# Decayed keys made token-major by VectorE block transposes and a pass through HBM, in a hybrid encoder block

## The chip, the core and the metric

The kernel runs on one core of a Trainium2 chip. The core has TensorE (matrix products, written PE in the profile; its weight loads are PEld), VectorE (DVE), ScalarE (ACT), GpSimd (POOL) and SyncE (SP), which here issues the DMAs. Each engine works through its own instructions in order and waits on semaphores for the others. The metric is the device time of one execution in microseconds (us); less is better.

## What is computed

One layer of a bidirectional hybrid encoder on 1024 tokens of width 1024: gated linear attention (GLA) in both directions beside a pooling branch, both gated and merged, then a SwiGLU feed-forward part. The change touches the attention alone. Per head (4 heads, key width 128, value width 256) and direction:

```python
b = jnp.cumsum(log_a, axis=3)               # per chunk of tokens
q_e = q * jnp.exp(b)
k_e = k * jnp.exp(-b)
scores = jnp.einsum('bhncd,bhnsd->bhncs', q_e, k_e)   # masked afterwards
o_intra = jnp.einsum('bhncs,bhnse->bhnce', scores, v)
kv = jnp.einsum('bhnsd,bhnse->bhnde', k_d, v)         # k_d = k * exp(b_last - b)
# state: dec_n * state + kv_n, over the chunks in turn
o_inter = jnp.einsum('bhncd,bhnde->bhnce', q_e, s_in)
```

The backward direction is the same on reversed tokens without the diagonal, and both outputs are added. For `scores` the decayed keys are needed with the feature on the partitions (feature-major); for `kv` the sum runs over the tokens, so they are needed with the token on the partitions (token-major).

## The kernel before

**Precision.** Most products take float32 operands in two parts, a rounded high part and the rest as the low part. `split_to` (L199) makes them: a ScalarE copy to the high part (L200), a subtraction for the low part (L201). `products` (L270) then issues three matmuls for one product: high by high, high by low, low by high. So a product of token-major keys `kt` and values `v` needs the high part of `kt` for its first two matmuls and the low part for the third.

**The order.** All instructions are written out by hand in program order; nothing reorders them. The long projections (`feature_major`, L296, and others) form the main stream on TensorE. After each product of that stream `mm3` (L275) calls `pump` (L161), which lets side work go on: the generators put into `side` with `begin`, one of which is `attention(h)` (L813). Such a generator yields a number, the count of main-stream products of 512 columns that go by before its next piece. Head h+1's projections of q and k run on the main stream while head h's attention is at the side. Weight loads and jobs that prepare later weights hang on the same pump (`pending`, `aside`).

**A head's attention.** Tokens come in two halves of 512 (`half`), the direction is `d` (0 forward, 1 backward), and a (half, d) pair is called a group here. The groups are taken in the order (1,1), (0,1), (0,0), (1,0):

- `decay` (L842): VectorE subtracts, runs the cumulative sum (a scan of 512 columns) and takes off the chunks' totals.
- `exponentials` (L865): ScalarE makes the two exponentials and the factors.
- `apply_decay` (L876): VectorE writes the decayed keys `ke` (L881), GpSimd the decayed queries `qe`.
- `transposed_keys` (L896): TensorE transposes the four 128x128 blocks of `ke[half][:, d, :]` into one PSUM bank `kp` (L899), and `split_to` reads that bank into `kt` (L901).
- `advance` (L904): for one chunk n of 128 tokens, the product `kv` of `kt` and `value(n)`, then the running state on VectorE (`st`, L911 or L913) and its two scaled copies on ScalarE (`sb` or `sf`, L917; `so`, L921). The backward states go from n = 7 down to n = 1 (L967), with the first four steps on `kts[1, 1]` and the rest on `kts[0, 1]`; the forward states go up from n = 0 inside the loop at L985, on `kts[0, 0]` and from n = 4 on `kts[1, 0]`.
- `scores` (L924): the products of `ke` and `qe`, masked and split.

Where the four groups are transposed and split before: (1,1) at L954, three units after `apply_decay(0, 1)`; (0,1) at L959, 4.5 units later and 2.5 units ahead of step n = 7; (0,0) after step n = 3 (L976); (1,0) after the output of chunk 0 (L1005).

**Buffers.** `slots` is a pool of 39 buffers of 4 KB per partition, which a great many things share (`ke`, `qe`, `kt`, values, states, loaded tensors). PSUM has eight banks: three for the main stream, five (`ps_g`) for everything at the side, `kp` among it. `raw` is a ring of four buffers for loaded weights. All loads and stores are issued by SP, in program order, a waiting one ahead of all behind it.

## Time and profile before

| what | us |
|---|---|
| median of 3 runs (1374.78 to 1375.9) | 1375.06 |
| span of the profiled execution | 1373.4 |
| TensorE busy in the span | 1361.4 |
| VectorE, ScalarE, GpSimd busy | 836.8, 647.3, 752.1 |
| the 64 transposes into `kp`, busy on TensorE | 9.6 |
| first and last of them, start | 89.1 and 301.6 |

How to read the rows of the profile: `L273 PE MATMUL ps<-hh,wh` is line 273 of the kernel, the engine, the operation, and what it writes and reads by the program's names with buffer numbers left out. A row of a group ends with the busy time, the mean duration of one in ns and the engine's idle time ahead of them, with what ended it. A row of a timeline begins with the start and the duration in us; `x4` says that four like instructions are merged, and `[1.16 <-ACT kt L200]` that the engine stood idle for 1.16 us until ScalarE's instruction of that name. A row of windows gives the stretch, its length, the busy time of PE, PEld, DVE, ACT and POOL with their counts, the granted TensorE clock (1.00 is full), the busy share of the DMA engines, and GB/s. Rows of DMA issues give what is written and read, the count, the size of one, and the median us from issue to landing. SPq is SP's queue of DMA issues. Matmuls are pipelined and overlap, so their cost in the stream is read from the distance of starts.

### The profile page before, as it was taken

To read this page: it belongs to the slowest core of one execution; us is meant where nothing else is said; L and a number is where in the kernel's file an instruction comes from. 1 tells how busy PE (TensorE), PEld (TensorE's weight loads), DVE (VectorE), ACT (ScalarE), POOL (GpSimd) and SP (SyncE) were. 2 spreads that over 40 slices of the span, in tenths; PEclk is the share of its full clock that TensorE was granted. 3 is DMA by queue.
4 is the path that set the end of the run, shared out by engine and by line. 5 is a ranking of instruction groups with operands and counts; after the bars stand their busy time and mean duration, and the time that the engine had idled before them with its cause. 6 is when DMAs were issued, how large, how long until landed. Compare 5 with 4: busy or idle time off the path is not lost. (4 is left out here: it accounts for less than half of the span.)

```text
span 1373.4 us, 17879 instructions
## 1 busy us (share of the span) xinstructions
PE 1361.4 (99%) x6310; PEld 1132.9 (82%) x6310; DVE 836.8 (61%) x1034; ACT 647.3 (47%) x1177; POOL 752.1 (55%) x557
## 2 busy tenths in 40 slices
PE   9999999999999999999999999999999999999998
PEld 7888888888888888888888888888888888888886
DVE  6974556554735777678883955655566556343375
ACT  7365666755534445554346533333333334444253
POOL 3323723222597547667764376666676667455454
PEclk9999999999999999999999999999999999999999
DMA  6321523314778569995416355555544447985451
GB/s 227 113 87 52 181 90 92 95 60 123 245 236 278 186 198 308 373 386 216 150 71 241 112 174 176 176 176 177 176 145 137 146 136 266 384 301 187 169 215 77
DMA packets 167834, 251.97 MB, mean 183 GB/s; under 512 B 11160, under 2 KB 94144, under 8 KB 167744
## 3 DMA queue, kind: packets, MB, share of 16 engines
q1 hardware_dynamic: 167600, 250.57, 53.8%
q8 instruction: 49, 0.80, 0.2%
q14 instruction: 41, 0.34, 0.1%
q10 hardware_dynamic: 144, 0.26, 0.0%
HBM read 168.74 MB, written 82.05 MB: 183 GB/s over the span
## 5 line engine op out<-in xcount | busy, mean ns | idle before, releaser
L201 POOL TENSOR_TENSOR wl<-fs,wh 128x512 fp32r<-128x512 f32 x124 | 173.1, 1400 | 163.5 <-ACT wh L200 104.0
L273 PE MATMUL ps<-gh,wh 128*128 128x512 f32 x616 | 240.5, 390 | 0.0
L273 PE MATMUL ps<-gl,wh 128*128 128x512 f32 x616 | 239.8, 389 | 0.3 <-DVE gl L1691 0.3
L273 PE MATMUL ps<-gh,wl 128*128 128x512 f32 x616 | 239.7, 389 | 0.0
L201 POOL TENSOR_TENSOR wl<-fraw,wh 128x512 fp32r<-128x512 f32 x93 | 134.0, 1442 | 75.0 <-ACT wh L200 72.4
L201 POOL TENSOR_TENSOR ol<-gor,oh 128x1024 fp32r<-128x1024 f32 (+1 forms) x42 | 101.3, 2417 | 86.0 <-ACT oh L200 71.7
L273 PE MATMUL ps<-hh,wh 128*128 128x512 f32 x356 | 145.1, 408 | 0.7 <-ACT ga L1474 0.7
L273 PE MATMUL ps<-hh,wl 128*128 128x512 f32 x356 | 139.0, 390 | 0.0
L273 PE MATMUL ps<-hl,wh 128*128 128x512 f32 x356 | 138.8, 390 | 0.0
L273 PEld LDWEIGHTS ps<-gl,wh 128*128 128x128 f32 x616 | 115.7, 188 | 24.5 <-DVE gl L1691 0.7
L273 PEld LDWEIGHTS ps<-gh,wh 128*128 128x128 f32 x616 | 115.7, 188 | 24.1 <-ACT hb L1710 0.2
L273 PEld LDWEIGHTS ps<-gh,wl 128*128 128x128 f32 x616 | 115.7, 188 | 23.9
L273 PE MATMUL ps<-oh,oh 128*128 128x512 f32 x308 | 119.8, 389 | 0.0
L273 PE MATMUL ps<-ol,oh 128*128 128x512 f32 x308 | 119.8, 389 | 0.0
L273 PE MATMUL ps<-oh,ol 128*128 128x512 f32 x308 | 119.8, 389 | 0.0
L201 POOL TENSOR_TENSOR wl<-wraw,wh 128x512 fp32r<-128x512 f32 x56 | 92.3, 1679 | 44.7 <-ACT wh L200 44.6
L201 POOL TENSOR_TENSOR wl<-raw,wh 128x512 fp32r<-128x512 f32 x34 | 47.4, 1404 | 108.3 <-ACT wh L200 71.9
L201 DVE TENSOR_TENSOR ol<-wor,oh 128x1024 fp32r<-128x1024 f32 (+1 forms) x42 | 62.8, 1506 | 68.1 <-ACT oh L200 55.5
L200 ACT CAST wh<-fs 128x512 fp32r<-128x512 f32 x124 | 76.1, 615 | 29.5 <-DVE fs L1093 28.3
L273 PEld LDWEIGHTS ps<-hh,wl 128*128 128x128 f32 x356 | 66.8, 188 | 14.4
L273 PEld LDWEIGHTS ps<-hh,wh 128*128 128x128 f32 x356 | 67.0, 188 | 13.1 <-ACT ga L1474 1.1
L273 PEld LDWEIGHTS ps<-hl,wh 128*128 128x128 f32 x356 | 67.0, 188 | 12.0
(281 smaller groups left out, 3073.4 us busy)
## 6 DMA issues: line engine op xcount, KB each, us to landing
fraw<-in_w_ffn_in_dram SPq DMA_DIRECT2D x44, 512.0 KB, 6.1
gor<-g_out SPq DMA_DIRECT2D x35, 512.0 KB, 6.1
fraw<-in_w_in_dram SPq DMA_DIRECT2D x22, 512.0 KB, 6.5
g_out<-s SPq DMA_DIRECT2D x44, 256.0 KB, 2.3
wor<-t_out SPq DMA_DIRECT2D x20, 512.0 KB, 3.7
raw<-in_w_in_dram SPq DMA_DIRECT2D x36, 256.0 KB, 5.1
g_out<-g SPq DMA_DIRECT2D x33, 256.0 KB, 2.6
x<-in_x_dram SPq DMA_DIRECT2D x16, 512.0 KB, 5.6
```

Of the source, the lines that this page charges most:

```text
L200: nc.scalar.copy(hi, src)
L201: eng.tensor_tensor(lo, src, as_f32(hi), op=ALU.subtract)
L273: nc.tensor.matmul(ps, a[i], b[j], start=first and n == 0, stop=last and n == 2, skip_group_check=onto)
```

## The change

`transposed_keys` goes, and with it the 64 transposes on TensorE, the PSUM bank `kp` and the splits that read it. Four functions take its place:

- `turn_keys`: one VectorE transpose of 32x32 blocks over `ke[half][:, d, :]` (128 x 512) into the first half of a slot `kq`, with the blocks' columns rearranged on the way.
- `put_keys`: four DMAs, one for each 32 partitions, store that to a scratch tensor `k_out` in HBM, in rows of 512 bytes, so that the blocks land where a full transpose would have them.
- `get_keys`: one DMA loads the scratch tensor (128 x 512) into the second half of `kq`.
- `split_keys`: `split_to` from there into `kt`, with the columns put back into order on the way.

Each group's steps are spread over the schedule. `turn_keys` follows `apply_decay` of its group. The split of (1,1) moves to where (0,1) was transposed and split before, and that of (0,1) moves behind step n = 6; (0,0) and (1,0) are split where they were transposed before.

```diff
+SQ = 32
...
+    k_out = {
+        (h, half, d): dram.tile([P, HALF], F32, name=f"k_out{h}{half}{d}")
+        for h in range(HEADS) for half in range(2) for d in range(2)
+    }
...
-        def transposed_keys(half, d):
-            kp = bank(ps_g, "kp")
+        turned = {}
+
+        def turn_keys(half, d):
+            both = slot(s="kq")
+            nc.vector.transpose(
+                both[:, 0, :].rearrange("p (j c b) -> p c j b", j=4, b=SQ),
+                ke[half][:, d, :].rearrange("p (c j a) -> p c j a", j=4, a=SQ),
+            )
+            turned[half, d] = both
+
+        def put_keys(half, d):
+            to = k_out[h, half, d].rearrange("(j a) (i m) -> i a j m", a=SQ, i=4)
             for i in range(4):
-                nc.tensor.transpose(kp[:, i * P : (i + 1) * P], chunk_of(ke, 4 * half + i, d), ident[:, :])
+                src = turned[half, d][i * SQ : (i + 1) * SQ, 0, :]
+                nc.sync.dma_start(to[i], src.rearrange("p (j m) -> p j m", j=4))
+
+        def get_keys(half, d):
+            nc.sync.dma_start(turned[half, d][:, 1, :], k_out[h, half, d])
+
+        def split_keys(half, d):
             kt = slot(F32R, s="kt")
-            split_to(kt[:, 0, :], kt[:, 1, :], kp[:, :])
-            return kt
+            hi, lo = (kt[:, i, :].rearrange("p (c i b) -> p c i b", c=4, b=SQ) for i in range(2))
+            back = turned[half, d][:, 1, :].rearrange("p (i c b) -> p c i b", i=4, b=SQ)
+            split_to(hi, lo, back)
+            kts[half, d] = kt
...
+        kts = {}
         decay(1, 1)
         yield HOLD
         exponentials(1, 1)
...
         apply_decay(1, 1)
+        turn_keys(1, 1)
         yield HOLD - 2
         exponentials(0, 1)
         decay(0, 0)
+        put_keys(1, 1)
         yield 2
         apply_decay(0, 1)
+        turn_keys(0, 1)
         yield HOLD - 2
         exponentials(0, 0)
-        kts = {(1, 1): transposed_keys(1, 1)}
+        put_keys(0, 1)
+        get_keys(1, 1)
         yield 1.5
         apply_decay(0, 0)
         decay(1, 0)
+        turn_keys(0, 0)
         yield HOLD - 2
-        kts[0, 1] = transposed_keys(0, 1)
+        split_keys(1, 1)
         exponentials(1, 0)
+        get_keys(0, 1)
+        put_keys(0, 0)
         yield 2.5
...
             if n == 7:
                 apply_decay(1, 0)
+                turn_keys(1, 0)
+            elif n == 6:
+                split_keys(0, 1)
+                get_keys(0, 0)
+            elif n == 5:
+                put_keys(1, 0)
             yield 1.2
             if n == 3:
-                kts[0, 0] = transposed_keys(0, 0)
+                split_keys(0, 0)
+                get_keys(1, 0)
                 yield 0.5
...
             if n == 0:
                 yield 0.38
-                kts[1, 0] = transposed_keys(1, 0)
+                split_keys(1, 0)
```

## The prediction

> **What bounds the kernel now.** I read the page's busy times and chain of waits, then the windows of the four stretches in which the heads' keys are transposed, then the timelines of TensorE, VectorE, ScalarE and the DMA queue (SPq) there. Times are us from the start of the span.

> ```profile
> PE 1361.4 (99%) x6310; PEld 1132.9 (82%) x6310; DVE 836.8 (61%) x1034; ACT 647.3 (47%) x1177; POOL 752.1 (55%) x557
> PE 44%; DVE 1%; ACT 1%; issue 0%; POOLq 0%; POOL 0%; DVEq 0%; ACTq 0%
> 80.00:120.00 40.00, 40.00 (x222) 34.59 (x222) 24.67 (x45) 22.96 (x53) 17.37 (x16) 1.00 0.18 54
> 145.00:185.00 40.00, 39.08 (x217) 33.20 (x215) 22.32 (x41) 23.31 (x54) 24.80 (x22) 1.00 0.41 135
> ```

> TensorE is busy for 99% of the span, and in the first two heads' stretches for 40.00 and 39.08 of 40 us. So the program is one in-order stream of matmuls: what leaves that stream is gained, and each wait that enters it is lost, because nothing later gives it back. VectorE is busy 24.67 and 22.32 of 40 us there, the DMA engines 18% and 41%: room on average. Averages don't decide this change, though. The order within some ten microseconds of each head does.

> **What goes.** Per head four groups of four transposes leave TensorE, 16 groups in all.

> ```profile
> L899 PE MATMUL kp<-ident,ke 128*128 128x128 f32 x64 | 9.6, 272 | 0.0
> 88.45 0.62 PE L273 MATMUL ps<-wv,hh 128*128 128x512 f32 x2
> 88.90 0.40 PE L273 MATMUL ps<-wv,hl 128*128 128x512 f32 x1
> 89.14 0.60 PE L899 MATMUL kp<-ident,ke 128*128 128x128 f32 x4
> 89.50 0.70 PE L273 MATMUL ps<-wv,hh 128*128 128x512 f32 x2
> ```

> They never waited (0.0 idle), so their time is true TensorE time. What one group costs I read from starts, since ends overlap. A 512-wide matmul is normally followed after about 0.23 us (two of them and the next start: 88.45 to 88.90). With a group between, the next one starts 0.60 after 88.90, which is 0.37 more, and the pair after it takes 0.70 where 0.62 is normal: 0.45 us a group. Sixteen make **7.2 us**; the row's 9.6 us busy is the upper end, 16 x 0.37 = 5.9 the lower. The freed PSUM banks gain nothing more: TensorE waits for no bank there.

> **What is moved.** I name a group by (half, direction): (1,1), (0,1), (0,0), (1,0) in order. The split of (1,1) into `kt` stood right behind its transposes. It now stands where the split of (0,1) stood, because the round trip through HBM has to fit in between. But the first `kv` matmuls of a head (n = 7) use (1,1), and their place in TensorE's order is the same. The third of them needs the low part. So I compare, head by head, VectorE's low part of the *second* group with the third `kv` matmul:

> ```profile
> 95.45 0.68 DVE L201 TENSOR_TENSOR kt<-kp,kt 128x512 fp32r<-128x512 f32 x1
> 95.09 0.28 PE L273 MATMUL kv<-vh,kt 128*128 128x256 f32 x1
> 157.70 0.28 PE L273 MATMUL kv<-vh,kt 128*128 128x256 f32 x1
> 222.64 0.68 DVE L201 TENSOR_TENSOR kt<-kp,kt 128x512 fp32r<-128x512 f32 x1
> 222.05 0.28 PE L273 MATMUL kv<-vh,kt 128*128 128x256 f32 x1
> 284.79 0.68 DVE L201 TENSOR_TENSOR kt<-kp,kt 128x512 fp32r<-128x512 f32 x1
> 285.30 0.28 PE L273 MATMUL kv<-vh,kt 128*128 128x256 f32 x1
> ```

> Two groups leave TensorE ahead of these matmuls in each head, so it arrives 0.90 earlier: at 94.19, 156.80, 221.15 and 284.40. The low part at the new place ended at 96.13, 160.18 (row below), 223.32 and 285.47. Without any transfer or added VectorE work TensorE would already wait 1.9 + 3.4 + 2.2 + 1.1 = **8.6 us**, more than is saved.

> **What is added.** Per group: one VectorE transpose of 128x512, four stores of 64 KB, one load of 256 KB, and a split that reads SBUF in place of PSUM.

> ```profile
> L309 DVE TENSOR_SCALAR xn<-x,n1rs 128x1024 f32<-128x1024 f32 (+1 forms) x10 | 7.4, 746 | 4.2 <-POOL n1rs L305 4.1
> L851 DVE TENSOR_TENSOR_SCAN z<-carry,la 128x512 f32<-128x512 bf16 x8 | 14.2, 1772 | 0.3
> L201 DVE TENSOR_TENSOR wv<-vraw,wv 128x512 fp32r<-128x512 f32 x5 | 4.1, 821 | 0.0
> L200 ACT CAST wv<-vraw 128x512 fp32r<-128x512 f32 x8 | 4.8, 618 | 0.9 <-DMA vraw<-in_w_in_dram 0.9
> 116.36 0.34 SPq L694 DMA_DIRECT2D s_out<-wsum  x1
> g_out<-s SPq DMA_DIRECT2D x44, 256.0 KB, 2.3
> wl<-u_out SPq DMA_DIRECT2D x14, 256.0 KB, 3.3
> raw<-in_w_in_dram SPq DMA_DIRECT2D x36, 256.0 KB, 5.1
> ```

> - The transpose isn't in this trace. Bounds: 0.37 us (half of the SBUF scaling of 1024 columns) and 1.77 (the scan). I take 0.69, as for the other one-result-per-column operations of 512 (`ke`, `la`, the `kt` split), which is 0.61 in a full queue, where starts overlap by 0.08.
> - The split: 0.62 for the high part, 0.82 for the low part (the SBUF rows; from PSUM the low part was 0.69).
> - An issue on SP: 0.34, so about 0.37 each, 1.48 for a group's four stores. Load to landing: 2.3 to 5.1 us; I take 3.3, the row of a scratch tensor of the same 256 KB.

> [...]

> Now the path to the first low part, with head 1 in full, then the starts for the others:

> ```profile
> 152.95 0.68 DVE L881 TENSOR_TENSOR ke<-z,k 128x512 f32<-128x512 f32 x1
> 154.79 0.69 DVE L201 TENSOR_TENSOR kt<-kp,kt 128x512 fp32r<-128x512 f32 x1 [1.16 <-ACT kt L200]
> 155.40 0.68 DVE L881 TENSOR_TENSOR ke<-z,k 128x512 f32<-128x512 f32 x1
> 159.16 0.43 DVE L862 TENSOR_TENSOR z<-z,tot 128x256 f32<-128x256 f32 x1
> 159.50 0.68 DVE L201 TENSOR_TENSOR kt<-kp,kt 128x512 fp32r<-128x512 f32 x1
> 88.48 0.68 DVE L881 TENSOR_TENSOR ke<-z,k 128x512 f32<-128x512 f32 x1
> 216.41 0.68 DVE L881 TENSOR_TENSOR ke<-z,k 128x512 f32<-128x512 f32 x1
> 218.34 3.03 SPq L208 DMA_DIRECT2D raw<-in_w_in_dram  x2
> 277.56 0.68 DVE L881 TENSOR_TENSOR ke<-z,k 128x512 f32<-128x512 f32 x1
> ```

> SP runs in order, and the load of (1,1) is queued behind the stores of (0,1), which wait for (0,1)'s transpose. In head 1 `ke` of (0,1) ends at 153.63; two transposes (1,1 and 0,1) push this to 154.85; four stores, 156.33; load landed, 159.63; high part, 160.25; low part, 161.07. TensorE wanted it at 156.80: **4.3 us**. The same sum from 89.16, 217.09 and 278.24 gives 96.60, 224.92 (SP is at the first of two weight loads until 218.70, 0.39 later) and 285.68: waits of 2.4, 3.8 and 1.3. Together **11.8 us**. VectorE alone gives nearly the same in head 1: from 154.85 the queue `ke` to `z` of 4.19 (155.40 to 159.59), a third transpose and the low part end at 160.5. A faster transfer alone saves at most 0.6 there.

> The split of (0,1), moved behind step n = 6, waits next, on ScalarE.

> ```profile
> 159.63 0.60 ACT L871 ACTIVATE qe<-z 128x512 f32<-128x512 f32 x1 [1.42 <-DVE z L862]
> 160.64 0.19 ACT L873 ACTIVATE fac<-tot 128x8 f32<-128x8 f32 x1
> 160.73 0.50 ACT L917 ACTIVATE sb<-st,fac 128x256 f32<-128x256 f32 x1
> 161.13 0.50 ACT L921 ACTIVATE so<-st,fac 128x256 f32<-128x256 f32 x1
> 161.90 0.28 PE L273 MATMUL kv<-vh,kt 128*128 128x256 f32 x1
> 95.36 1.13 ACT L200 CAST wh<-raw 128x512 fp32r<-128x512 f32 x2
> ```

> ScalarE waits for the load in order, so behind the high part (160.25) come the exponentials of (1,0), 1.20 (159.63 to 160.83), then `sb`/`so` of n = 7, 0.90, after `st`; another `st` (some 0.5) and pair, then high and low part of (0,1): about 165.5. Its third matmul (161.90) stands 4.20 behind that of n = 7, so at 165.27: 0.25 us more. In head 0 two weight casts (1.13, last row) stand there too: 1.0 by the same sum. I put about 0.5 on each of heads 2 and 3: **2.2 us** in all. (0,0) and (1,0) have ten units of the schedule or more between load and split and cost nothing; were that cover gone, they would cost like (0,1).

> Queued behind SP's new waits are loads of weights and of `wsum`, and stores. I cost them at nothing: four `raw` buffers, and TensorE itself stands meanwhile. `kq` needs one or two of 39 slots at a time and comes free before the slots get short.

> **Sum.** 1373.4 (span of the profiled execution) - 7.2 + 11.8 + 2.2 = 1380.2. The median of the runs, 1375.06, lies 1.7 above that span, so **1382 us**, 0.5% slower.

> **Rivals.**

> 1. *Hidden (faster).* The low part is there in all heads and only the saving counts: 1375.06 - 7.2 = 1368. For it: VectorE and the DMA engines have room on average. Against it: the 8.6 us by which the new place was late before anything was added. It decides only if VectorE stands idle enough ahead of the split; the 1.16 us idle in head 1's rows goes into the added transposes. 0.10.
> 2. *Balance.* A transpose at 0.37 and a landing at 2.3 us take 0.64 + 1.0, and a low part of 0.69 another 0.13, off each path, 1.8 a head and 1.3 in head 3, together 6.7: 1375. 0.13.
> 3. *Slow transfers.* Stores and `raw` loads both move 512-byte rows; if the load lands after 5.1 us behind its own stores, each head loses 1.8 more: 1382 + 7.2 = 1389, and some weights late behind SP. 0.13.
> 4. *Clock.* In the row below TensorE is idle and the granted clock averages 0.67. A wait that long in heads 1 and 2 could halve the clock for as long again, some 1.7 us of loss each: 1385. 0.04.

> ```profile
> 1368.40:1373.40 5.00, 0.00 (x0) 0.00 (x0) 0.75 (x1) 0.72 (x1) 0.37 (x1) 0.67 0.34 128
> ```

> [...]

> **Chances and range.** Forecast, 1378 to 1387 for itself: 0.60. A run of this kernel tells about 0.2% from no change (1372.3 to 1377.8). Faster 0.10 (rival 1), same 0.13 (rival 2), slower 0.77 (the rest). The range leaves out rival 1 and the far end of rival 3: 1373 to 1391.

> **What would show it.** In the profile after: no `kp`; TensorE waiting in front of `kv`, named by `kt`'s casts and differences, 1 to 4 us in each head, most in heads 1 and 2; ScalarE idle in front of `kt`, ended by the DMA into `kq`; 16 transposes on VectorE near 0.69 us; the busy time of TensorE some 7 us shorter. I'm wrong if `kv` starts without waits (the path is shorter than summed), if the load lands after 2.3 us and VectorE is never full, or if the waits sit at weights (`wl`), which would mean SP's queue did the harm.

## The result, and the profile after

Each time is a median of runs on one chip.

| | before | after |
|---|---|---|
| time | 1374.9 us (1374.7 to 1375.9) | **1392.3 us** (1391.8 to 1392.8) |
| ratio | | 1.0125, 95% interval 1.0110 to 1.0139 |
| span of the profiled execution | 1373.4 us | 1390.7 us |

The forecast was 1382 us, with a range to 1391. The sign was right. The loss is 17.4 us, where 7 were forecast.

From the page of the changed kernel the busy times; from the view of its groups by form (line, engine, operation, count; busy us, mean ns; idle before) the new ones; from the view of DMA issues the trip (count, KB, median us to landing):

```profile
PE 1361.9 (98%) x6246; PEld 1130.0 (81%) x6246; DVE 846.7 (61%) x1050; ACT 647.4 (47%) x1177; POOL 753.4 (54%) x557
```

```profile
L905 DVE STREAM_TRANSPOSE kq<-ke 128x512 f32<-128x512 f32 x16 | 11.3, 709 | 1.2 <-POOL qe L887 0.6
L202 DVE TENSOR_TENSOR kt<-kq,kt 128x512 fp32r<-128x512 f32 x16 | 12.5, 780 | 32.9 <-ACT kt L201 31.4 <-DMA s_out<-wsum 1.5
```

```profile
k_out<-kq SPq DMA_DIRECT2D x64, 64.0 KB, 1.8
kq<-k_out SPq DMA_DIRECT2D x16, 256.0 KB, 3.5
```

The 64 transposes are gone from TensorE (6310 matmuls became 6246), yet its busy time is no shorter: some of the others ran longer. The new operations cost what was forecast: the transpose 0.71 us (0.69), the low part 0.78 (0.82), a load 3.5 from issue to landing (3.3).

The two stretches of the first heads again (TensorE, its loads, VectorE, ScalarE, GpSimd busy; granted clock, DMA share), then the view of waits from 80 to 340 us, which spans the four heads (us in total, times, longest):

```profile
80.00:120.00 40.00, 37.85 (x199) 31.86 (x198) 26.63 (x49) 21.84 (x50) 16.01 (x15) 1.00 0.38 112
145.00:185.00 40.00, 29.81 (x139) 24.83 (x138) 20.51 (x35) 19.41 (x42) 26.20 (x23) 0.87 0.66 191
```

```profile
PE kv L274 <- ACT kt L201: 15.0, 3, 10.0
PE kv L274 <- DVE kt L202: 1.7, 6, 0.6
ACT kt L201 <- DMA kq<-k_out: 11.3, 3, 4.6
ACT kt L201 <- POOL fac L888: 7.3, 1, 7.3
```

In the second stretch TensorE fell from 39.08 to 29.81 us busy, at a clock of 0.87. Over the four heads three waits for the high part of `kt` make 15.0 us, and one of them alone, in head 1, is 10.0 us.

The other matmuls run in the same order in both kernels, so they can be paired. Over all pairs TensorE idles 16.7 us more. It saves 0.43 to 0.46 us at each of the 16 places where a group of transposes went, 7.2 in all. The span grew by 17.3 us, so the rest, 17.3 - 16.7 + 7.2 = 7.8 us, are matmuls that follow each other more slowly. Some 5 of these lie from 168 to 176 and from 236 to 244 us, behind the long waits of heads 1 and 2, where the granted clock is 0.50 to 0.86.

**Head 1.** SP's queue, one ScalarE row and TensorE's rows of n = 7 (start, us, engine, line, operation, count, and in brackets the idle time before it):

```profile
152.02 0.82 SPq L757 DMA_DIRECT2D raw<-in_w_in_dram  x1
152.94 3.49 SPq L915 DMA_DIRECT2D k_out<-kq  x4
159.39 0.34 SPq L695 DMA_DIRECT2D s_out<-wsum  x1
159.83 1.84 SPq L915 DMA_DIRECT2D k_out<-kq  x4
161.84 0.34 SPq L918 DMA_DIRECT2D kq<-k_out  x1
...
167.43 0.62 ACT L201 CAST kt<-kq 128x512 fp32r<-128x512 f32 x1 [7.33 <-POOL fac L888]
...
168.10 0.58 PE L274 MATMUL kv<-vh,kt 128*128 128x256 f32 x1 [9.99 <-ACT kt L201]
169.10 0.58 PE L274 MATMUL kv<-vh,kt 128*128 128x256 f32 x1 [0.20 <-DVE kt L202]
```

The transpose of (0,1) was done at 155.9, but its four stores went out only at 159.83. A store of `s_out` stood ahead of them and waited for one of GpSimd's sums until 159.39. So the load of (1,1) was issued at 161.84; the forecast had 156.33. The high part began at 167.43, which is 5.6 us after the issue, where 3.3 was forecast. So the high part came 7.8 us later than forecast. TensorE itself came 1.4 us later, and its wait grew from 4.3 to 10.2 us. The releaser named at 167.43, GpSimd's `fac`, had ended at 167.27, but nothing in the split needs it. Of the DMAs whose semaphores it waits for, two came last by the counts in the trace: the load, which was complete at 164.97, 3.1 us after its issue, and the store to `s_out` issued at 162.22, complete at 167.27. That store reads the `wsum` tile in whose slot this `kt` is put. So the slot held the split up for 2.3 us more than the load did.

### The profile page after: what moved, and what is told of

Its sections match the earlier page's. It is cut to its first block, busy times and chain, and to the rows that moved or that the text cites. A ratio compares the mean times of both kernels' runs of the same rounds, so it can differ in the third digit from the quotient of the medians.

```text
span 1390.7 us, 17914 instructions
## 1 busy us (share of the span) xinstructions
PE 1361.9 (98%) x6246; PEld 1130.0 (81%) x6246; DVE 846.7 (61%) x1050; ACT 647.4 (47%) x1177; POOL 753.4 (54%) x557
## 5 line engine op out<-in xcount | busy, mean ns | idle before, releaser
L274 PEld LDWEIGHTS ps<-gl,wh 128*128 128x128 f32 x616 | 115.7, 188 | 24.4 <-DVE gl L1729 0.7
L201 ACT CAST wh<-fs 128x512 fp32r<-128x512 f32 x124 | 76.1, 615 | 29.5 <-DVE fs L1131 28.5
## 6 DMA issues: line engine op xcount, KB each, us to landing
g_out<-s SPq DMA_DIRECT2D x44, 256.0 KB, 2.5
raw<-in_w_in_dram SPq DMA_DIRECT2D x36, 256.0 KB, 4.0
g_out<-g SPq DMA_DIRECT2D x33, 256.0 KB, 2.6
```

The source lines that it names most:

```text
L201: nc.scalar.copy(hi, src)
L274: nc.tensor.matmul(ps, a[i], b[j], start=first and n == 0, stop=last and n == 2, skip_group_check=onto)
```

## The experiments

Sixteen kernels were run, each timed in three rounds beside the kernel before. The base of a run is "before" (1375.0) or, where the branch jobs begin a head later, e12 (1373.3).

| run | what it is | us | ratio to before, 95% | less its base |
|---|---|---|---|---|
| e1 | after, without the round trip | 1389.4 | 1.0085 to 1.0116 | +14.4 |
| e2 | all added steps, `kt` still from TensorE | 1385.2 | 1.0058 to 1.0092 | +10.2 |
| e3 | (1,1) on TensorE, the rest by trip | 1394.7 | 1.0129 to 1.0159 | +19.7 |
| e4 | branch jobs run faster | 1392.4 | 1.0111 to 1.0141 | +17.4 |
| e5 | head 1's and 2's waits filled | 1392.1 | 1.0108 to 1.0138 | +17.0 |
| e9 | `kt`'s slot taken early | 1392.6 | 1.0114 to 1.0149 | +17.4 |
| e10 | e1 and e9 together | 1393.3 | 1.0117 to 1.0147 | +18.1 |
| e12 | before, branch jobs later | 1373.3 | 0.9978 to 0.9997 | base |
| e11 | after, branch jobs later | 1389.4 | 1.0090 to 1.0120 | +16.1 (e12) |
| e13 | e11 without the round trip | 1382.1 | 1.0037 to 1.0071 | +8.8 (e12) |
| e16 | e13, first split at its old place | 1386.8 | 1.0068 to 1.0098 | +13.5 (e12) |
| e17 | e12 and 16 unused transposes on VectorE | 1376.4 | 1.0000 to 1.0020 | +3.1 (e12) |
| e15 | e11, load and split of (1,1) earlier | 1397.7 | 1.0150 to 1.0181 | +24.4 (e12) |
| e6 | only (0,0) and (1,0) by trip | 1383.6 | 1.0048 to 1.0078 | +8.7 |
| e14 | e6, branch jobs later | 1386.1 | 1.0063 to 1.0093 | +12.8 (e12) |
| e18 | e6 with one `kq` tile for both groups | 1382.1 | 1.0034 to 1.0067 | +7.1 |

### Is it the round trip? (e1 to e4)

The first theory was that head 1's transfer, late behind SP's queue, makes the waits. Four runs took parts away.

```diff
 e1: put_keys and get_keys do nothing
-            back = turned[half, d][:, 1, :]
+            back = turned[half, d][:, 0, :]
 e2: transposed_keys at its four old places, split_keys nowhere
 e3: turn, put and get of (1,1) removed
+        kts[1, 1] = transposed_keys(1, 1)
 e4:
-            prepare_beside(map(branch_jobs, range(4)), 4.2)
+            prepare_beside(map(branch_jobs, range(4)), 1.6)
```

> Leaves out the round trip: the split reads the block-transposed keys as they stand, so blocks stay in the wrong place. VectorE's transposes and the later places of the splits stay. [...] If the later place and VectorE's full queue make them, as the forecast's 8.6 us say, at least 8 us of waits stay and the time is 1380 us or more.

> All that is added is there (transposes on VectorE, stores, loads), but the keys are taken from TensorE's transposes at the old places as before. If the waits for kt are the whole loss, this is 1375 to 1377 us. If the added work and traffic themselves slow other things (weights late behind SP, VectorE's queue), it is 1380 us or more and the waits lie in front of other matmuls than kv.

> Only group (1,1) goes back to TensorE at its old place; the other three make the trip. If the wait at the first kv of each head is the loss (17 us of it, and 3.6 us of half clock behind it), this is 1372 to 1379 us: the saving of 12 groups, 5.4 us, less some 1 to 4 us of waits for (0,1). If the wait only moves on to (0,1) at n = 3, head 1 waits 5 us or more there and the time is 1382 us or more.

> The side jobs that load and store sums of the branch weights run every 1.6 units in place of 4.2, so that they are through SP's queue before head 1's keys. If a store of such a sum in front of the keys' stores, and the loads behind them, made head 1's wait 10 us in place of 4, this is 1382 to 1387 us with head 1's wait at 4 to 5 us. If the keys' own path makes it, head 1 still waits 9 to 10 us and the time stays within 1390 to 1394.

Without any transfer 14 of the 17 us stayed, and e2 lost 10 with its keys made as before. The theory fell. e3 and e4 only moved the wait: 10.7 us at n = 3 in e3, 12.7 at n = 7 in e4. Head 1 of e1, on ScalarE and VectorE, then e2's waits between 150 and 180 us:

```profile
162.30 0.62 ACT L201 CAST kt<-kq 128x512 fp32r<-128x512 f32 x1 [3.69 <-DMA s_out<-wsum]
170.00 0.71 DVE L905 STREAM_TRANSPOSE kq<-ke 128x512 f32<-128x512 f32 x1 [4.52 <-POOL qe L887]
```

```profile
ACT kt L201 <- DMA s_out<-wsum: 5.9, 1, 5.9
ACT sb L948 <- POOL qe L887: 3.7, 1, 3.7
```

Neither `kt` nor `kq` nor `sb` reads `wsum` or `q`. They wait for the *slot*. The addresses of the tiles in the built program say so: in e1, head 1's first `kt` lies where a `wsum` tile lay whose store is only just going out, and the `kq` of (1,0) lies where `q` lay, which GpSimd still reads.

### Is it the slots? (e9, e10, e6, e18)

```diff
 e9, e10:
         def put_keys(half, d):
+            if d == 1:
+                kts[half, d] = slot(F32R, s="kt")
+                nc.scalar.copy(kts[half, d][:, 0, :1], ke[half][:, d, :1])
 e6: (1,1) and (0,1) by transposed_keys at their old places
 e18, on e6: turn_keys(1, 0) at n == 5 and not at n == 7
-            both = slot(s="kq")
+            both = turned[0, d] if half else slot(s="kq")
```

> The changed kernel; at the place of put_keys of the two backward groups, (1,1) and (0,1), the slot of their kt is taken at once by a one-column copy on ScalarE (8 small copies in all; split_keys then writes the rest). In the kernel as changed, head 1's kt(1,1) takes the slot that a wsum tile has just left, and its first copy must wait until that tile's store has gone out, which waits for GpSimd's sum; here it takes the slot of a value tile whose last reader was 91 matmuls earlier. Theory A (the 16 extra kq slots in a pool of 39 make kt wait for wsum's stores): the wait of ScalarE put down to fac or to s_out<-wsum ahead of head 1's first split goes; as the trip of that group lands at about 165.3 and the split began at 167.4, head 1's wait at n=7 falls from 10.8 to about 8.8 us, no more, and the time from 1392.3 to about 1390. Rival B (the slots are nothing, the loss is the trip and what stands ahead of it in SP's queue): head 1's wait stays at 10.8 within 0.5 and the time at 1392.

> The kernel without the round trip (e1_no_trip, which measured 1389.4; the round trip is left out, the split reads the transposed half where it lies), with the slots of kt(1,1) and kt(0,1) taken early as in e9_early_kt. No load, and no slot just left by a wsum tile, stands before head 1's split. Theory A: head 1's waits (6.1 us at n=7, 3.5 at n=3) and the half clock behind them go, and with them some 10 to 14 us: 1375 to 1379 if the waits of heads 0 and 2 stay, down to 1368 if all go. Rival B: nothing of it changes, 1389 within 1.

> The kernel before (1375, the branch jobs at their old place) with only the forward groups (0,0) and (1,0) by VectorE and the trip; (1,1) and (0,1) on TensorE as before. Saves half, 3.6 us, on TensorE. Theory F: the transposes of (0,0) and (1,0) still stand in VectorE's stretch ahead of n=7 and n=6, 1.4 us a head, and the loads' waits in SP's queue hold up what stands behind them, as in e14_two_late (12.5 us over its base): 1374 to 1384. Rival (e14's loss came from the branch jobs that ran in heads 2 and 3 with it): 1371 to 1373.

> e6_two_by_trip (1383.6) with one kq tile for both forward groups: (1,0) is transposed into the half of (0,0)'s tile that its stores have left, at n=5 in place of n=7, right ahead of its stores. 4 kq slots in place of 8. In e6, head 1's transpose of (1,0) stood 7.4 us on VectorE (161.6 to 169.0), for its slot was that of q, which GpSimd read until 168.97, and TensorE lost 5.2 us at the next kv and 2 behind it. Theory A (slots): that wait goes and the kernel falls by 5 to 7 us, to 1377 to 1379; not lower if the transposes in VectorE's stretch and the forward waits stay. Rival (the wait is GpSimd's or SP's being late and shows elsewhere, whichever slot is taken): 1382 or more, with ScalarE's sb or a kt waiting for q or wsum instead.

e9: the split began at 165.40 in place of 167.43, 3.1 us behind the issue of its load in place of 5.6, as the semaphores of the changed kernel had it. But ScalarE then waited 4.8 us for the slot of an `sb`, and nothing was gained. Head 1 of e10, of e6 (three engines) and of e18 (two):

```profile
173.32 0.51 ACT L939 ACTIVATE sb<-st,fac 128x256 f32<-128x256 f32 x1 [9.78 <-POOL qe L887]
```

```profile
167.72 1.25 POOL L887 TENSOR_TENSOR qe<-qe,q 128x512 f32<-128x512 f32 x1
169.01 0.71 DVE L913 STREAM_TRANSPOSE kq<-ke 128x512 f32<-128x512 f32 x1 [7.37 <-POOL qe L887]
170.14 0.58 PE L274 MATMUL kv<-vh,kt 128*128 128x256 f32 x1 [5.34 <-DVE st L944]
```

```profile
167.08 1.28 POOL L887 TENSOR_TENSOR qe<-qe,q 128x512 f32<-128x512 f32 x1
168.40 0.51 ACT L948 ACTIVATE sb<-st,fac 128x256 f32<-128x256 f32 x1 [3.93 <-POOL qe L887]
```

One late slot, that of `q`, goes round. In e6 it falls to the transpose of (1,0), which starts 0.04 us after GpSimd's last read of `q`; the states queue behind it on VectorE, and TensorE loses 5.3. e18 gives that transpose another tile, and the slot falls to the lower `sb`; TensorE then waits 3.6 us at a later product (`op` at 176.19). e18 regained 1.5 us of the 5 to 7 expected: whoever comes next pays. In the kernel before, a tile with room took this slot:

```profile
169.22 0.59 ACT L200 CAST kt<-kp 128x512 fp32r<-128x512 f32 x1 [1.69 <-POOL qe L882]
```

That is the `kt` of (0,0), needed some 8 us later. So the pool was already short before the change, but where that hurt nobody.

### Without the branch jobs in head 1 (e11, e12, e13)

```diff
 e11, on after; e12, on before; e13, on e1
-            prepare_beside(map(branch_jobs, range(4)), 4.2)
         if h == 2:
+            prepare_beside(map(branch_jobs, range(4)), 4.2)
             value_weights.pop().products()
```

> The changed kernel with the jobs of the branch weights (loads into wsum, GpSimd's sums, stores s_out) begun a head later, at the place where head 2 is projected, so that head 1's attention runs with neither their slots nor their stores in SP's queue. To be read against e12_before_jobs_late. Theory A and its kin (slots or SP's queue, either way by wsum's stores): head 1's wait of 10.8 falls to what the trip alone costs, below 5 us, and its half clock goes; part may come again in head 2 and 3, where the jobs now run. The difference to e12 falls from 17.4 to 8 to 13. Rival C (the trip alone is too slow for its place): head 1's wait stays above 9 and the difference to e12 at 17.

> The kernel before with the jobs of the branch weights begun a head later, as in e11_jobs_late: the base for that run. Expected 1375 to 1380 by all theories; the jobs must be done before the output stage, and may run late there.

> The round trip left out (the split reads the transposed half where it lies, as in e1_no_trip at 1389.4) and the branch jobs a head later (as in e12_before_jobs_late, the base, at 1373.3). Neither run alone got below 1389: e1 kept the slots short, so that kt waited for a wsum tile and kq and sb for a q tile that GpSimd still read; e11 kept the trip. Theory E (two waits stand side by side, the trip's and the slots', and either alone costs most of the loss): with both gone the kernel is the base less the saving on TensorE, 1373.3 - 7.1 = 1366, or up to 1370 if the lower parts now made from SBUF are late at places. Rival D (the new steps' places in the order of VectorE and ScalarE cost the time themselves, whatever they wait for): 1378 or more.

Head 1 of e11 (SP, ScalarE, TensorE), and n = 7 of its head 2:

```profile
152.53 6.62 SPq L915 DMA_DIRECT2D k_out<-kq  x8
159.32 1.53 SPq L918 DMA_DIRECT2D kq<-k_out  x2
162.08 0.62 ACT L201 CAST kt<-kq 128x512 fp32r<-128x512 f32 x1 [3.29 <-DMA kq<-k_out]
162.75 0.39 PE L274 MATMUL kv<-vh,kt 128*128 128x256 f32 x1 [4.29 <-ACT kt L201]
...
231.14 0.39 PE L274 MATMUL kv<-vh,kt 128*128 128x256 f32 x1 [3.83 <-ACT kt L201]
```

Here the forecast's chain can be seen without the store of `s_out` in head 1, and its sizes come out nearly: waits of 4.29 and 3.83 us, and 0.22 more at the third matmul of each, where 4.3 and 3.8 stood in it. In head 1 that is partly luck: the load was issued 0.8 us after TensorE would have wanted the third matmul, where 0.5 ahead was forecast, and landed after 2.7 us in place of 3.3. In the kernel as changed head 1 had 10.2. Yet the loss hardly fell, from 17.4 to 16.1. Paired with their bases, head 1 loses 4.6 us less than in the changed kernel, and heads 2 and 3, where the `wsum` loads and sums now ran, 4.0 more.

e13 takes the trip away as well. Of its head 1, ScalarE's high part, VectorE's queue behind it, and TensorE:

```profile
157.19 0.63 ACT L201 CAST kt<-kq 128x512 fp32r<-128x512 f32 x1
...
157.08 2.13 DVE L856 TENSOR_TENSOR_SCAN z<-carry,la 128x512 f32<-128x512 bf16 x1
159.79 0.70 DVE L905 STREAM_TRANSPOSE kq<-ke 128x512 f32<-128x512 f32 x1
160.42 0.65 DVE L202 TENSOR_TENSOR kt<-kq,kt 128x512 fp32r<-128x512 f32 x1
...
161.12 0.39 PE L274 MATMUL kv<-vh,kt 128*128 128x256 f32 x1 [2.75 <-DVE kt L202]
```

The high part is there at 157.8. The low part waits until 160.42 behind the scan and the third transpose, and TensorE waits for it, with neither a transfer nor a short slot in play. The base less the saving would be 1366.1; e13 is 16.0 us above that, the larger part of e11's 23.3. This bears out rival D. It also bears out the forecast's own 8.6 us for the later place alone: over the four heads e13's waits at n = 7 come to 8.9.

### VectorE's stretch (e16, e17, e15)

```diff
 e16, on e13
         get_keys(1, 1)
+        split_keys(1, 1)
         yield 1.5
...
-        split_keys(1, 1)
         exponentials(1, 0)
 e17, on e12: four turn_keys at the changed kernel's places, results unused
 e15, on e11: split_keys(1, 1) and then get_keys(0, 1) ahead of apply_decay(0, 0), and
         yield 2
+        get_keys(1, 1)
         apply_decay(0, 1)
```

> e13_no_trip_late (1382.1, round trip left out) with split_keys(1,1) where transposed_keys(1,1) stood before: ahead of apply_decay(0,0), decay(1,0) and turn_keys(0,0) on VectorE. In e13 the upper part of kt(1,1) was made at 157.2 in head 1, but its lower part only at 160.4, behind those steps on VectorE, and TensorE waited 2.7 us for it. Theory F (VectorE's own stretch, from the keys' arrival to the state behind n=5, sets the time; whatever is put in it, or moved in it, comes out at its end): the waits at n=7 go (3.6, 2.9, 1.0 us in heads 1 to 3) but the state of n=7 is later, and n=3 waits for most of it: 1378 to 1382. Rival G (the place of that one split is the loss): 1373 to 1375.

> The kernel before with the branch jobs a head later (base e12_before_jobs_late, 1373.3) and the 16 transposes on VectorE at their new places, their result unused: no trip, no new split, kt from TensorE at the old places. Adds 16 x 0.71 us on VectorE and 16 short-lived slots. Theory F: three of four stand in the stretch of VectorE that the backward chain waits for, 2.1 us a head; heads with no room lose about that: 1376 to 1382. Rival G: VectorE is busy 61% and hides them: 1373 to 1374.

> e11_jobs_late (1389.4) with the load of (1,1) issued ahead of the stores of (0,1), right behind its own stores, and with split_keys(1,1) ahead of apply_decay(0,0) on VectorE, and the load of (0,1) ahead of the stores of (0,0). In e11 the stores of (1,1) had landed by 156 in head 1 and its load was issued at 159.3, behind the stores of (0,1). Theory E: the loads come about 3 us earlier, the waits at n=7 fall from 3.9, 3.9 and 1.0 in heads 1 to 3 to about 1, and with them the half clock behind them: 1379 to 1384. Rival C (the trip's own duration is the bound, whatever stands ahead of it): 1388 or more.

The first row is TensorE in e16's head 1 (n = 3), then come VectorE and TensorE (n = 4) in e17's:

```profile
166.57 0.58 PE L274 MATMUL kv<-vh,kt 128*128 128x256 f32 x1 [3.51 <-ACT kt L201]
```

```profile
160.16 0.70 DVE L898 STREAM_TRANSPOSE kq<-ke 128x512 f32<-128x512 f32 x1
160.78 0.65 DVE L201 TENSOR_TENSOR kt<-kp,kt 128x512 fp32r<-128x512 f32 x1
161.49 0.38 PE L273 MATMUL kv<-vh,kt 128*128 128x256 f32 x1 [0.56 <-DVE kt L201]
```

With the split at its old place the waits at n = 7 are gone, but the state of n = 7 then comes behind the scan and the transpose on VectorE, the split of (0,1) behind that, and n = 3 waits 3.5 and, in head 2, 4.5 us. So the waits moved, as the theory of the stretch had it: paired with e13, whose profiled span is 5.2 us shorter, e16 waits only 0.5 us more in all. The other 4.7 us are matmuls that follow each other more slowly, most of them at half clock behind the waits at n = 3. The windows show head 1 of e16, then of e13:

```profile
168.00:172.00 4.00, 4.00 (x12) 3.23 (x12) 0.97 (x2) 2.90 (x7) 0.48 (x1) 0.50 0.09 35
```

```profile
168.00:172.00 4.00, 4.00 (x25) 3.53 (x24) 1.49 (x3) 2.34 (x6) 1.20 (x1) 1.00 0.17 66
```

e17 adds 16 transposes to VectorE, and the slots that they write, and costs 3.1 us. In its row above n = 4 waits because its product takes the PSUM bank that `kp` of (0,1) held, and the split that reads `kp` stands behind the transpose. Paired with e12, head 1 loses 1.1 us and head 2 loses 1.9, where three transposes of 0.7 us stand in each. So this stretch, from the keys' arrival to the states of n = 7 to 5, has little room in heads 1 and 2, though VectorE is busy 61%. e15 missed most: in head 1 the load went out 3.5 us sooner behind its stores, and the waits at n = 7 fell below 1.3 us, but those at n = 3 grew to 2.3, 3.6, 6.1 and 3.4, as in e16.

### The clock, and SP's queue (e5, e14)

```diff
 e5, ahead of the backward chain of heads 1 and 2
+            for i in range((0, 84, 34)[h]):
+                nc.tensor.transpose(idle[:, ...], ident[:, :], ident[:, :])
 e14: e6 with the branch jobs begun at h == 2
```

> The changed kernel with 84 and 34 transposes of the identity on TensorE, their result unused, ahead of the backward chain of heads 1 and 2, where TensorE stood still for about 10 and 4 us and then ran at a granted clock of 0.50 to 0.58 and 0.75 for some us. The waits are as long as before, only filled. If the half clock comes from standing still, its 1.7 and 1.9 us go: 1388.7 (1388 to 1390), and the granted clock in the windows behind the waits is 0.9 or more. If not, or if the clock goes down by what runs in other engines, 1392 or more.

> The backward groups (1,1) and (0,1) by TensorE as before, the forward groups (0,0) and (1,0), which have 10 us and more of room, by VectorE and the trip, and the branch jobs a head later (base e12_before_jobs_late, 1373.3). Theory E: half of the saving on TensorE, 3.6 us, and no wait at the backward chain, since its keys come as before: 1369.7, or up to 1372 with small waits at the forward keys. Rival D: 1375 or more.

Windows of head 1, after and then e5 (granted clock third from the end):

```profile
164.00:168.00 4.00, 0.00 (x0) 0.00 (x0) 0.00 (x0) 0.57 (x2) 4.00 (x6) 0.50 1.02 290
168.00:172.00 4.00, 3.70 (x11) 3.02 (x12) 2.60 (x4) 2.06 (x6) 4.00 (x5) 0.50 0.74 255
```

```profile
164.00:168.00 4.00, 3.83 (x36) 3.59 (x33) 0.00 (x0) 0.08 (x1) 4.00 (x7) 1.00 0.94 271
168.00:172.00 4.00, 2.67 (x14) 2.20 (x15) 2.29 (x3) 2.55 (x6) 4.00 (x4) 1.00 0.90 312
```

Filling the wait kept the clock at 1.00, and the time did not change: TensorE, now faster, waited the more for `kt` and the states (2.67 of 4 us busy where it had been 3.70). The half clock is real, but here it fills time in which TensorE would have waited. Whether that holds for e16 too was not tried.

e14 missed by 14 us. A row of head 3 on ScalarE, then e14's waits from 225 to 320 us, which span heads 2 and 3:

```profile
301.58 0.62 ACT L201 CAST wh<-raw 128x512 fp32r<-128x512 f32 x1 [3.97 <-DMA raw<-in_w_in_dram]
```

```profile
PE op L274 <- ACT p L201: 5.3, 2, 4.2
PE sc L960 <- DVE st L944: 3.5, 1, 3.5
```

In each of the two heads a weight load came late, its cast held up ScalarE (4.8 us in head 2, 4.0 in head 3), and `kt`, the states and `p` came behind it. The load shares SP's queue with the trip's waits; which of them held it up was not taken apart.

## Why the prediction was wrong

- **The saving (7.2 us): right**, 0.43 to 0.46 us a group.
- **Durations: right.** By their semaphores the loads of (1,1) landed 2.6 to 3.1 us after their issue in the four heads. Only the issue of a store was longer, 0.44 us where 0.37 stood. The transpose of a group took 0.71 us, where 0.69 stood.
- **The waits at n = 7 (11.8 us): the mechanism right, head 1 mis-sized.** After shows 1.5, 10.2, 3.9 and below 0.5 us in heads 0 to 3, where 2.4, 4.3, 3.8 and 1.3 were forecast; e11 shows 4.3 and 3.8 in heads 1 and 2. The claim that VectorE alone would give nearly the same in head 1 is borne out by e13: 0.8 and 2.8 us there without any transfer.
- **The step that failed first: SP's queue.** The forecast put only the stores of (0,1) ahead of the load of (1,1). A store of `s_out` that waits for GpSimd's sum stands there too; the row from which the forecast took the price of an issue, 116.36, is such a store. In head 1 the load's issue was 5.5 us late: the transpose of (0,1) was done 1.0 later than forecast, 3.9 more passed before its first store went out, most of them behind that store of `s_out`, and the four stores took 0.5 longer.
- **The step that failed with it: "`kq` ... comes free before the slots get short", at nothing.** Slots are short in head 1. There the `kt` of (1,1) got the slot of a `wsum` tile, and its high part began 2.5 us after the load had landed, 2.3 of them until the last store out of that tile was complete. With the 5.5 us above, and 0.2 that the load was faster, that is the 7.8 us by which the high part was late. e6 prices one such wait by itself, 7.4 us on VectorE and 5.3 on TensorE. The short slots lie beside the late load, which is why neither removing the trip (e1) nor moving the slot (e9) brought the time back.
- **The wait at n = 3 (2.2 us)** came out at 0.6 in head 0 and at most 0.2 in the others. The forward chain adds 0.3 and 0.4 us in head 1 and 0.6 in head 3, ahead of `kv` and `op`, where nothing was forecast.
- **The sum** had 14.0 us of waits, and the trace has 16.7. The larger miss in it is the 7.8 us of matmuls that follow each other more slowly, for which it had no term.
- **Rival 4, the clock (0.04),** did happen: head 1's and head 2's waits were followed by 0.50 and 0.75. Its row of the kernel before, which averages 0.67, has the clock fall from 1.00 to 0.50 at 1370.10 us, 2.99 us behind the end of TensorE's last matmul, and stay there for the 3.3 us to the end of the span, 1.7 us of loss. As a price it fell in e5 for these two waits; in e16 up to 4.7 us may be its price. Rival 3, slow transfers, did not come: in head 1 the load landed 3.1 us after its issue, and what was late was its issue and the slot. Rival 2 needed a transpose of 0.37 us and a load of 2.3, and neither came. Rival 1, that all is hidden, was wrong in every run.

What remains open is how the whole loss divides, since its causes stand side by side. The runs bound it from two sides. With the branch jobs out of head 1 (e13, e11), the new steps without the trip cost 16.0 us before the saving, and the trip 7.3 more, though the jobs in heads 2 and 3 may add to both. With the jobs at their old place, the steps without the trip cost 21.6 (e1), and the trip 2.9 more.

No version of the change beat the kernel before. The only faster one, e12, is the kernel before with the branch jobs a head later: 1373.3 us, 0.1% faster.

## What to carry to other kernels

An engine that is busy 61% can have next to no room in the ten microseconds that matter: list its queue from the arrival of the data to the result that the bound engine waits for, and price each new step there at its full time. A tile from a shared pool is not free because it is short-lived; it shifts which tile gets the slot that comes free last, so look up who held each slot before. Of a queue that runs in order, list what else is in it, with what each entry waits for, before you place a dependent store and load there.

## What the runs showed of the hardware

```profile
228.00:232.00 4.00, 3.92 (x22) 3.35 (x22) 2.85 (x7) 1.91 (x6) 1.33 (x2) 1.00 0.70 197
```

```profile
232.00:236.00 4.00, 4.00 (x15) 3.39 (x16) 2.82 (x6) 1.98 (x7) 1.10 (x2) 0.57 0.91 273
```

```profile
101.00:104.50 3.50, 3.50 (x11) 2.88 (x10) 0.97 (x2) 2.81 (x7) 0.00 (x0) 0.51 0.06 17
```
